# One bias for two heads: the row maxima of the latent softmax scaled and clamped in pairs

## The chip, the core and the metric

The kernel runs on one core of a Trainium2 chip. The metric is the device time of one execution in microseconds. Three runs of the kernel before gave 1462.78, 1457.17 and 1461.98 us: a median of 1461.98 us. One further execution was profiled; every duration below is from that one, which took 1457.81 us with a span of 1455.8 us.

## The reference, cut to what matters

One layer of a hybrid network works on 128 context tokens and 512 latent tokens, width 1024. One input projection feeds a two-way RWKV scan (branch A) and a windowed attention with 16 query heads in 4 groups, each group with its own keys and values (branch B); two output projections, sigmoid gates and a last projection merge them. The part in question is the attention of the latent queries, in blocks of 128 queries:

```python
def one(i):                                   # block i of 4
    s_loc = einsum('bhgqd,bhkd->bhgqk', qi, ki) * ATTN_SCALE      # window of up to 384 keys, masked
    s_ctx = einsum('bhgqd,bhkd->bhgqk', qi, k_ctx) * ATTN_SCALE   # 128 context keys
    pr = _sink_softmax(jnp.concatenate([s_loc, s_ctx], axis=-1), sink)
    return pr[..., :KSPAN] @ vi + pr[..., KSPAN:] @ v_ctx
```

The softmax has one extra column, the learned sink of the head, in its sum. The exponent is taken of the score less a maximum, so each row needs `-max(scale * row maximum, sink)` as its bias before the exponential can start.

## The kernel before, in words

All operations are recorded by one helper (line 138), so the trace shows one line for all and they are told apart by the names of their tiles. The scan and the input projections take the time to about 1106 us and are ordered by hand. What follows (from line 1603) is left to a list scheduler, which orders each engine's instructions by priority and by its own idea of their durations; the order is fixed when the program is built, and each engine then works strictly in that order.

From line 1623 a loop goes over the four head groups. For a group, `attend` (line 1293) makes the scores of its four heads against the context (one block, tile `Pc`), then four blocks of latent queries (tile `Pl`): blocks 0 and 3 have 384 keys, blocks 1 and 2 have 512. For each head of a block (line 1348): TensorE makes the scores in a PSUM tile `ur`, of which there are two (line 193), from the high and low parts of the keys (`KH`, `KL`) with queries `qt`, and adds the band mask with an identity product (`amask`, `identb`). VectorE takes the row maximum into one column of `nm` (line 1358), and scales and clamps it (line 1359); ScalarE reads `ur`, makes the exponential into `Pl` and its row sums in `ssum` (line 1364). Only then is that `ur` tile free for the head after next.

After four heads `softmax_tail` (line 1297) makes the reciprocals `den`, scales the four `Pl` on VectorE, and then for each 128 keys TensorE turns the four heads' pieces into one PSUM tile `sc` (a set of four transposes), ScalarE copies it out (`PT`), and TensorE multiplies it with the values (into `st` or `mi`). There is one `sc` tile, so a set waits for the copy of the set before. A group has 15 sets: one for the context block and 3, 4, 4 and 3 for the latent blocks; four groups have 60.

Two streams share the engines. Keys and queries of the next group are prepared in groups 0 to 2 (rotations `sh`, `R`, `us_q`, splits `qt`). And the projection of branch A (`branch_a`, 8 column blocks of 48 products, tiles `g` from `ah`, `al`, `wh`, `wl`) has the lowest priority: its products are the filler of TensorE. Two PSUM tiles `g` hold the two halves of a column block until VectorE has emptied them with `stg<-us_ma,g`; `us_ma` is loaded on SP's queue. After the attention, `branch_b` needs the gated outputs `bh`, `bl` of all groups (`yb` times `us_gb`, cast on ScalarE, low part on POOL), and `output` ends the kernel.

Of the kernel before, what the change touches and what calls it, by code (L numbers as in the profile page):

```python
# [15 lines left out]
AF = mybir.ActivationFunctionType  # L16
ALU = mybir.AluOpType
# [17 lines left out]
SCALE = 0.125  # L35
# [134 lines left out]
def hybrid_step(ctx, tc, a):  # L170
    nc = tc.nc
    clock = Clock()
    act, dve, pool_e, pe = (Timed(e, k, clock) for e, k in (
        (nc.scalar, "act"), (nc.vector, "dve"), (nc.gpsimd, "pool"), (nc.tensor, "pe")))
# [8 lines left out]
    def T(shape, tag, bufs, dt=F32, name=None):  # L183
        bufs = NB.get(tag, bufs)
        return sb.tile(shape, dt, tag=tag, name=name or tag, bufs=bufs)
# [6 lines left out]
    def PUR():  # L192
        return pools["ur"].tile([P, 512], F32, tag="ur", name="ur", bufs=2)
# [4 lines left out]
    def PSC():  # L198
        return psp.tile([P, 512], F32, tag="sc", name="sc", bufs=1)
# [15 lines left out]
    for tb in range(5):  # L215
# [13 lines left out]
                      in1=pv[:, :16].rearrange("p (c k) -> p c k", c=2), op=ALU.mult)  # L229
# [101 lines left out]
    for c in range(2):  # L331
        dve.tensor_tensor(out=mTf[:, c, :], in0=mTf[:, c, :], in1=vec("b_ada", 0, 16), op=ALU.add)
        dve.scalar_tensor_tensor(out=mTf[:, c, 8:16], in0=mTf[:, c, 8:16], scalar=1.0, in1=vec("norm_w", 0, 8),
                                 op0=ALU.add, op1=ALU.mult)
# [3 lines left out]
    for k in range(KB):  # L338
        hi = T([P, TOK], "h", 16, F32R, name="hh")
        for c, (t0, t1) in enumerate(((0, CTX), (CTX, TOK))):  # L340
            dve.tensor_scalar(out=xT[k][:, t0:t1], in0=xT[k][:, t0:t1], scalar1=mTf[:, c, 8 + k:9 + k],
                              scalar2=mTf[:, c, k:k + 1], op0=ALU.mult, op1=ALU.add)
# [203 lines left out]
    def unspill(nm, b, tag, bufs):  # L546
        t = T([P, TOK], tag, bufs, name="us_" + nm)
        nc.sync.dma_start(out=t, in_=spills[nm, b])
        return t
# [743 lines left out]
    def attend(g, Q, KH, KL, vt_, cv):  # L1293
        yb = [T([P, TOK], t, 1, name="yb") for t in ("bv", "DG")]
        hs = slice(4 * g, 4 * g + 4)

        def softmax_tail(Ps, nm, ssum, nk, vals, col0):
            den = T([P, 4], "den", 2, name="den")
            dve.tensor_tensor(out=den, in0=nm, in1=sink[:, hs], op=ALU.add)
            act.activation(out=den, in_=den, func=AF.Exp)  # L1300
            dve.tensor_tensor(out=den, in0=den, in1=ssum, op=ALU.add)
            dve.reciprocal(out=den, in_=den)
            for j in range(4):
                dve.tensor_scalar(out=Ps[j], in0=Ps[j], scalar1=den[:, j:j + 1], scalar2=None, op0=ALU.mult)
            po = (PST, PMI)[alt[0] % 2]()
            alt[0] += 1
            for kb in range(nk):
                pt = PSC()
                for j in range(4):
                    pe.transpose(out=pt[:, j * P:(j + 1) * P], in_=Ps[j][:, kb * P:(kb + 1) * P], identity=ident)  # L1310
                PT = T([P, 4, P], "SB", 10, name="PT")
                act.copy(out=PT.rearrange("p j x -> p (j x)"), in_=pt)
                for half in range(2):
                    pe.matmul(out=po[64 * half:64 * half + 64, 0:256], lhsT=vals[kb], rhs=PT[:, half::2, :],
                              start=(kb == 0), stop=(kb == nk - 1))
            for b in range(2):
                dve.tensor_copy(out=yb[b][:, col0:col0 + P], in_=po[:, b * P:(b + 1) * P])


        nm = T([P, 4], "nm", 2, name="nm")  # L1320
        ssum = T([P, 4], "ssum", 2, name="ssum")
        Ps = [None] * 4
        ps = PUR()
        for j in range(4):
            o = ps[:, j * P:(j + 1) * P]
            pe.matmul(out=o, lhsT=Q[j][:, 0:CTX], rhs=KH[:, 6 * P:], start=True, stop=False)
            pe.matmul(out=o, lhsT=Q[j][:, 0:CTX], rhs=KL[:, 6 * P:], start=False, stop=True)
        dve.tensor_reduce(out=nm, in_=ps.rearrange("p (j x) -> p j x", j=4), axis=AX.X, op=ALU.max)
        dve.scalar_tensor_tensor(out=nm, in0=nm, scalar=-SCALE, in1=nsink[:, hs], op0=ALU.mult, op1=ALU.min)
        Pt = T([P, 4, P], "S", 5, name="Pc")  # L1330
        for j in range(4):
            Pj = Pt[:, j]
            act.activation(out=Pj, in_=ps[:, j * P:(j + 1) * P], func=AF.Exp, scale=SCALE,
                           bias=nm[:, j:j + 1], accum_out=ssum[:, j:j + 1])
            Ps[j] = Pj
        softmax_tail(Ps, nm, ssum, 1, [vt_[0][:, CH * g:CH * g + CH]], 0)


        for i in range(4):
            b0, b1 = max(0, i - 1), min(3, i + 1)  # L1340
            nl = b1 - b0 + 1
            W = (nl + 1) * P
            c0 = 0 if i < 2 else P + P * b0
            f0 = P if i < 2 else 0
            nm = T([P, 4], "nm", 2, name="nm")
            ssum = T([P, 4], "ssum", 2, name="ssum")
            Ps = []
            for j in range(4):
                qs = Q[j][:, CTX + P * i:CTX + P * i + P]
                ps = PUR()  # L1350
                pe.matmul(out=ps[:, 0:W], lhsT=qs, rhs=KH[:, c0:c0 + W], start=True, stop=False)
                pe.matmul(out=ps[:, 0:W], lhsT=qs, rhs=KL[:, c0:c0 + W], start=False, stop=False)
                if i > 0:
                    pe.matmul(out=ps[:, f0:f0 + P], lhsT=identb, rhs=amask[:, 0, :], start=False, stop=(i == 3))
                if i < 3:
                    f1 = f0 + (nl - 1) * P
                    pe.matmul(out=ps[:, f1:f1 + P], lhsT=identb, rhs=amask[:, 1, :], start=False, stop=True)
                dve.tensor_reduce(out=nm[:, j:j + 1], in_=ps[:, 0:W], axis=AX.X, op=ALU.max)
                dve.tensor_scalar(out=nm[:, j:j + 1], in0=nm[:, j:j + 1], scalar1=-SCALE,
                                  scalar2=nsink[:, 4 * g + j:4 * g + j + 1], op0=ALU.mult, op1=ALU.min)  # L1360
                if j % 2 == 0:
                    Pt = T([P, 2, W], "S", 5, name="Pl")
                Pj = Pt[:, j % 2]
                act.activation(out=Pj, in_=ps[:, 0:W], func=AF.Exp, scale=SCALE, bias=nm[:, j:j + 1],
                               accum_out=ssum[:, j:j + 1])
                Ps.append(Pj)
            vals = [vt_[1 + b][:, CH * g:CH * g + CH] for b in range(b0, b1 + 1)]
            vals.insert(0 if i < 2 else nl, cv[:, g, :])
            softmax_tail(Ps, nm, ssum, nl + 1, vals, CTX + P * i)

        for b in range(2):
            sg = unspill("gb", 2 * g + b, "E", 1)
            if g < 3:
                bt = T([P, 2, TOK], ("bk", "ar", "ar")[g], 2, F32R, name="bt")
                bh, bl = bt[:, 0, :], bt[:, 1, :]
            else:
                bh = T([P, TOK], ("kk", "cs")[b], 1, F32R, name="bh")
                bl = T([P, TOK], ("rkv", "tmp")[b], 1, F32R, name="bl")
            dve.scalar_tensor_tensor(out=yb[b], in0=yb[b], scalar=0.5, in1=sg, op0=ALU.mult, op1=ALU.mult)
            act.copy(out=bh, in_=yb[b])  # L1380
            pool_e.tensor_tensor(out=bl, in0=yb[b], in1=bh.bitcast(F32), op=ALU.subtract)
            bhl.append((bh, bl))
# [230 lines left out]
    nsink = T([P, 16], "var", 1, name="nsink")  # L1613
# [9 lines left out]
    for g in range(4):  # L1623
        (KH, KL), Q = nxt
        if g < 3:
            nxt = whole(k_side(g + 1, kp)), whole(q_side(g + 1))
        attend(g, Q, KH, KL, vt_, cv)
        base = tc.cur_priority
        tc.cur_priority = 2000000 + base
        for _ in range(NBA[g]):  # L1630
            next(ba, None)
        tc.cur_priority = base + 2000
# [56 lines left out]
```

## Time and profile before

| what | value |
| --- | --- |
| runs, median (lowest to highest) | 1461.98 us (1457.17 to 1462.78) |
| profiled execution, its span | 1457.81 us, 1455.8 us |
| busy in the span: PE / DVE / ACT / POOL | 89% / 55% / 47% / 31% |
| attention, from its first score product to its last value product | 1106.7 to 1319.2 us |
| granted clock of the span | 0.952 of full speed |

PE is TensorE, PEld its weight loads, DVE VectorE, ACT ScalarE, POOL GpSimd, SP the queue that issues most transfers. A busy TensorE here means that a product was in the pipeline, not that the array was full. A waiting time in square brackets in a timeline is the idle time of the engine before the instruction and what ended it.

### The profile page before, as it was taken

The numbers are of one execution on the slowest core, as the hardware profiler recorded it, in microseconds if no ns is written. First come the engines' busy times: TensorE is split into PE (matmuls) and PEld (weight loads), VectorE is DVE, ScalarE is ACT, GpSimd is POOL, SyncE is SP. The second block draws the span as 40 slices with busy tenths as digits, with TensorE's granted clock in tenths as the row PEclk, the third lists the DMA queues.
The fourth block names the chain that finished last, engine by engine and source line by source line (L and its number), as shares of the span: only waits on it lengthen the run. The fifth ranks groups of instructions, "written<-read, shape, count | busy, mean of one in ns | idle before, by whom it ended". The sixth has DMA issues, their size and how long they took to land.

```text
span 1455.8 us, 40281 instructions
## 1 busy us (share of the span) xinstructions
PE 1301.2 (89%) x16959; PEld 1075.5 (74%) x16959; DVE 799.1 (55%) x1818; ACT 677.0 (47%) x1655; POOL 456.3 (31%) x476
## 2 busy tenths in 40 slices
PE   5699999989998999999998999999874789998996
PEld 0499888878887888887887887888553466777985
DVE  2436743665574475575465455437237787653447
ACT  2335364356356437436545645643433456553222
POOL 0333343224233233433332333332232122226330
PEclk9699999999999999999999999999885799999999
DMA  9133312223321321322231241233453222225532
GB/s 327 40 122 119 123 55 71 88 60 93 116 69 58 107 86 59 123 83 63 76 118 55 67 134 52 68 128 115 161 160 88 78 65 60 78 62 183 150 109 94
DMA packets 156722, 144.29 MB, mean 99 GB/s; under 512 B 16691, under 2 KB 130550, under 8 KB 156542
## 3 DMA queue, kind: packets, MB, share of 16 engines
q1 hardware_dynamic: 146632, 131.51, 28.9%
q10 hardware_dynamic: 9910, 10.21, 2.2%
q8 instruction: 133, 2.18, 0.6%
q14 instruction: 47, 0.39, 0.1%
HBM read 105.50 MB, written 36.18 MB: 97 GB/s over the span
## 4 chain that ended last, share of the span: by engine, by line
PE 69%; DVE 11%; issue 7%; ACT 5%; POOL 2%; DMA 1%; SPq 0%; DVEq 0%; ACTq 0%; POOLq 0%
PE g L138 39%; PE mi L138 11%; PE sc L138 7%; PE st L138 7%; PE ur L138 5%; DVE X L138 2%; DVE M L138 2%; ACT SB L138 1%; DVE Pl L138 1%; DVE St L138 1%; DVE o L138 1%; ACT L138 1%; DMA sp_rkv<-stg 1%; DVE stg L138 0%; DVE nm L138 0%
## 5 line engine op out<-in xcount | busy, mean ns | idle before, releaser
L138 POOL TENSOR_TENSOR wl<-wr,wh 128x512 fp32r<-128x512 f32 x170 | 229.2, 1352 | 637.7 <-ACT wh L138 599.2
L138 PE MATMUL g<-hh,wh 128*128 128x320 f32 (+1 forms) x1104 | 375.8, 340 | 9.9 <-DVE stg L138 4.9
L138 PE MATMUL g<-hl,wh 128*128 128x320 f32 (+1 forms) x1104 | 346.2, 314 | 5.1 <-issue 3.6
L138 PE MATMUL g<-hh,wl 128*128 128x320 f32 (+1 forms) x1104 | 345.7, 313 | 0.0
L138 PEld LDWEIGHTS g<-hh,wh 128*128 128x128 f32 x1104 | 210.8, 191 | 32.0 <-issue 7.8
L138 PEld LDWEIGHTS g<-hl,wh 128*128 128x128 f32 x1104 | 211.0, 191 | 5.7 <-issue 2.7
L138 PEld LDWEIGHTS g<-hh,wl 128*128 128x128 f32 x1104 | 211.8, 192 | 0.6
L138 ACT CAST wh<-wr 128x512 fp32r<-128x512 f32 x170 | 104.1, 618 | 17.3 <-PE g L138 11.3
L138 ACT COPY SB<-st 64x128 f32<-64x128 f32 x160 | 41.5, 260 | 144.0 <-PE st L138 142.8
L138 DVE SCALAR_TENSOR_TENSOR St<-St,pc,st 128x64 f32<-128x64 f32 x128 | 30.2, 277 | 124.1 <-PE st L138 100.3
L138 DVE SCALAR_TENSOR_TENSOR stg<-g,vt,stg 128x127 f32<-128x127 f32 (+1 forms) x144 | 60.8, 436 | 63.7 <-ACT stg L138 61.2
L138 ACT COPY U<-st 128x128 f32<-128x128 f32 x80 | 21.3, 266 | 136.4 <-DVE St L138 116.8
L138 POOL TENSOR_TENSOR S<-S,smask 128x512 f32<-128x512 f32 x40 | 50.8, 1271 | 98.9 <-ACT S L138 94.7
L138 PE MATMUL mi<-ar,bk 64*64 64x64 f32 (+1 forms) x960 | 71.9, 248 | 5.0 <-DVE XT L138 2.7
L138 ACT COPY SB<-sc 64x256 f32<-64x256 f32 (+1 forms) x160 | 55.2, 372 | 37.6 <-PE sc L138 36.4
L138 PEld LDWEIGHTS mi<-ar,bk 64*64 64x64 f32 (+1 forms) x960 | 61.9, 157 | 6.9 <-issue 2.9
L138 DVE TENSOR_TENSOR U<-ur,U 128x128 f32<-128x128 f32 x72 | 20.8, 289 | 77.3 <-PE ur L138 69.5
L138 ACT COPY PT<-sc 128x512 f32<-128x512 f32 x60 | 35.1, 584 | 47.9 <-PE sc L138 47.7
L138 DVE TENSOR_REDUCE nm<-ur 128x1 f32<-128x384 f32 (+2 forms) x68 | 41.4, 622 | 28.3 <-PE ur L138 28.0
L138 ACT ACTIVATE Pl<-ur,nm 128x384 f32<-128x384 f32 (+1 forms) x64 | 40.6, 635 | 28.1 <-DVE nm L138 25.5
L138 DVE TENSOR_TENSOR S<-sc,smask 128x512 f32<-128x512 f32 x40 | 27.3, 683 | 45.8 <-PE mi L138 24.9
L138 PE MATMUL g<-bt,wh 128*128 128x320 f32 x192 | 46.7, 320 | 5.3 <-DVE stg L138 5.3
(284 smaller groups left out, 2920.1 us busy)
## 6 DMA issues: line engine op xcount, KB each, us to landing
wr<-in_w_in SPq DMA_DIRECT2D x138, 256.0 KB
sp_rkv<-stg SPq DMA_DIRECT2D x48, 160.0 KB
rkv<-sp_rkv SPq DMA_DIRECT2D x24, 320.0 KB
wa_t<-in_w_ada SPq DMA_DIRECT2D x11, 512.0 KB
wg<-in_w_ada SPq DMA_DIRECT2D x16, 256.0 KB
wr<-in_w_oA SPq DMA_DIRECT2D x16, 256.0 KB
wr<-in_w_oB SPq DMA_DIRECT2D x16, 256.0 KB
wo<-in_w_out SPq DMA_DIRECT2D x16, 256.0 KB
```

The source lines that it names most:

```text
L138: return f(**kw)
```

## The change

The bias of two heads is made by one instruction. The maxima of heads 0 and 1 are taken first, then one `scalar_tensor_tensor` scales and clamps both columns of `nm`, then both exponentials follow; heads 2 and 3 likewise. The context block is as before (there all four columns were one instruction already), and so is everything else that the program asks for.

```diff
                 dve.tensor_reduce(out=nm[:, j:j + 1], in_=ps[:, 0:W], axis=AX.X, op=ALU.max)
-                dve.tensor_scalar(out=nm[:, j:j + 1], in0=nm[:, j:j + 1], scalar1=-SCALE,
-                                  scalar2=nsink[:, 4 * g + j:4 * g + j + 1], op0=ALU.mult, op1=ALU.min)
+                two.append(ps)
                 if j % 2 == 0:
                     Pt = T([P, 2, W], "S", 5, name="Pl")
-                Pj = Pt[:, j % 2]
-                act.activation(out=Pj, in_=ps[:, 0:W], func=AF.Exp, scale=SCALE, bias=nm[:, j:j + 1],
-                               accum_out=ssum[:, j:j + 1])
-                Ps.append(Pj)
+                    continue
+                dve.scalar_tensor_tensor(out=nm[:, j - 1:j + 1], in0=nm[:, j - 1:j + 1], scalar=-SCALE,
+                                         in1=nsink[:, 4 * g + j - 1:4 * g + j + 1], op0=ALU.mult, op1=ALU.min)
+                for b in range(2):
+                    act.activation(out=Pt[:, b], in_=two.pop(0)[:, 0:W], func=AF.Exp, scale=SCALE,
+                                   bias=nm[:, j - 1 + b:j + b], accum_out=ssum[:, j - 1 + b:j + b])
+                    Ps.append(Pt[:, b])
```

The scheduler answers with another order on every engine from the first group on. Three places of it matter below.

VectorE, in group 0, behind the rotation of the queries for group 1 (the piece begins with it); `nm` holds the maxima of latent block 0, `Pc` is the context block's softmax, `R` the keys of group 1:

```order
 L138 TENSOR_TENSOR us_q<-t_14965,sh 128x512
 L138 RECIPROCAL den<-den 128x4
-L138 TENSOR_SCALAR nm<-nm,nsink 128x1
-L138 TENSOR_SCALAR Pc<-Pc,den 128x128 x4
+L138 SCALAR_TENSOR_TENSOR nm<-nm,nsink 128x2
+L138 STREAM_SHUFFLE sh<-R 128x512
+L138 TENSOR_SCALAR Pc<-Pc,den 128x128
 L138 TENSOR_TENSOR qt<-us_q,qt 64x640 x2
```

The single bias becomes the pair's, and one rotation and the two query splits now stand ahead of three of the four scalings of the context block.

TensorE, in group 1, ahead of the four transposes of latent block 0 (`sc<-ident,Pl`); `g<-ah` and `g<-al` are products of branch A:

```order
 L138 MATMUL g<-al,wh 128x320
+L138 MATMUL g<-ah,wh 128x320
+L138 MATMUL g<-ah,wl 128x320
+L138 MATMUL g<-al,wh 128x320
+L138 MATMUL g<-ah,wh 128x320
+L138 MATMUL g<-ah,wl 128x320
+L138 MATMUL g<-al,wh 128x320
+L138 MATMUL g<-ah,wh 128x320
```

This piece is the head of a run: fifteen products of branch A stand now where one stood, between the scores of the next block's first two heads and the first transpose.

TensorE, at the end of group 3, the sets of its last blocks:

```order
 L138 MATMUL sc<-ident,Pl 128x128 x4
-L138 MATMUL g<-al,wh 128x320
-L138 MATMUL g<-ah,wh 128x320
-L138 MATMUL g<-ah,wl 128x320
-L138 MATMUL g<-al,wh 128x320
-L138 MATMUL g<-ah,wh 128x320
 L138 MATMUL mi<-PT,vtok 64x256 x2
 L138 MATMUL sc<-ident,Pl 128x128 x4
```

Here five products of branch A stood between a set of transposes and the values of the set before; now none does, at this place and in all the sets behind it.

## Rows read from the trace of the kernel before

**Rows 1.** Stretches, one per head group: length; busy PE, PEld, DVE, ACT, POOL; clock; DMA.

```profile
1106.70:1183.20 76.50, 50.62 (x258) 31.89 (x259) 63.25 (x155) 36.67 (x94) 16.98 (x11) 0.74 0.22 66
1183.20:1229.70 46.50, 41.66 (x248) 27.26 (x247) 36.47 (x95) 26.58 (x70) 14.16 (x10) 0.93 0.17 51
1229.70:1276.70 47.00, 45.99 (x302) 32.98 (x301) 31.17 (x92) 27.91 (x76) 12.14 (x9) 1.00 0.30 89
1276.70:1319.20 42.50, 41.99 (x280) 30.36 (x280) 21.86 (x67) 20.62 (x50) 8.30 (x6) 1.00 0.30 94
```

**Rows 2.** Groups by shape, 1106 to 1310 us, VectorE: busy us, mean ns | idle before.

```profile
L138 DVE TENSOR_REDUCE nm<-ur 128x1 f32<-128x512 f32 x32 | 21.6, 684 | 17.8 <-PE ur L138 17.8
...
L138 DVE TENSOR_SCALAR nm<-nm,nsink 128x1 f32<-128x1 f32 x64 | 11.9, 206 | 0.3
```

**Rows 3.** The same view for ScalarE.

```profile
L138 ACT ACTIVATE Pl<-ur,nm 128x512 f32<-128x512 f32 x32 | 22.0, 688 | 18.8 <-DVE nm L138 16.9 <-DVE den L138 1.8
...
L138 ACT ACTIVATION_READ_ACCUMULATOR Pl<-ur,nm 128x1 f32 x64 | 12.7, 198 | 0.0
```

**Rows 4.** Instructions on the tile nm: ns min/median/max of one.

```profile
L138 DVE SCALAR_TENSOR_TENSOR nm<-nm,nsink x4: 152/162/165, 1112.6 to 1267.2; 128x4 f32<-128x4 f32 x4
```

**Rows 5.** Waits of TensorE, 1106 to 1325 us: total, times, longest.

```profile
PE ur L138 <- ACT Pl L138: 10.9, 8, 5.5
```

**Rows 6.** Timeline of TensorE, full clock: values and transposes, without filler, then with.

```profile
1173.30 0.65 PE L138 MATMUL mi<-PT,vtok 128*64 128x256 f32 x4 [0.64 <-ACT PT L138]
1173.88 0.66 PE L138 MATMUL sc<-ident,Pl 128*128 128x128 f32 x4
1174.29 0.31 PE L138 MATMUL ur<-KH,qt 128*128 128x128 f32 x1
...
1175.21 0.65 PE L138 MATMUL mi<-PT,cv 128*64 128x256 f32 x4
...
1314.39 0.65 PE L138 MATMUL mi<-PT,vtok 128*64 128x256 f32 x4
...
1316.31 0.65 PE L138 MATMUL mi<-PT,vtok 128*64 128x256 f32 x4
```

**Rows 7.** Timeline of TensorE: values and transposes at half clock, two branch A products.

```profile
1145.49 1.12 PE L138 MATMUL mi<-PT,cv 128*64 128x256 f32 x4
1146.55 1.12 PE L138 MATMUL sc<-ident,Pl 128*128 128x128 f32 x4
...
1288.09 0.31 PE L138 MATMUL g<-al,wh 128*128 128x320 f32 x1
1288.23 0.31 PE L138 MATMUL g<-ah,wh 128*128 128x320 f32 x1
```

**Rows 8.** Timeline of VectorE, scaling of block 0 in group 1.

```profile
1187.46 4.54 DVE L138 TENSOR_SCALAR Pl<-Pl,den 128x384 f32<-128x384 f32 x4
```

**Rows 9.** Stretches around three thin places; columns as in rows 1.

```profile
1134.00:1144.00 10.00, 6.35 (x27) 3.86 (x25) 9.38 (x24) 3.98 (x11) 4.09 (x3) 0.84 0.29 85
1144.00:1151.00 7.00, 6.43 (x24) 3.27 (x24) 4.59 (x12) 2.32 (x7) 0.30 (x1) 0.57 0.00 0
1186.00:1192.00 6.00, 3.02 (x17) 1.64 (x15) 5.08 (x8) 2.05 (x5) 4.79 (x4) 0.92 0.35 107
1192.00:1198.20 6.20, 6.14 (x24) 4.33 (x24) 5.72 (x13) 3.24 (x7) 2.60 (x2) 0.53 0.30 86
1202.00:1208.00 6.00, 4.75 (x25) 2.44 (x25) 5.40 (x17) 2.81 (x7) 1.14 (x1) 1.00 0.01 3
```

**Rows 10.** Timeline of TensorE: first late set of group 3, then the end.

```profile
1294.28 0.28 PE L138 MATMUL sc<-ident,Pl 128*128 128x128 f32 x1
...
1318.50 0.65 PE L138 MATMUL mi<-PT,cv 128*64 128x256 f32 x4
...
1325.37 0.64 PE L138 MATMUL g<-bt,wh 128*128 128x320 f32 x1 [5.29 <-DVE stg L138]
...
1332.83 0.41 PE L138 MATMUL g<-bl,wh 128*128 128x320 f32 x1 [1.32 <-POOL bl L138]
```

More of the change, by code (lines that the diff above doesn't have):

```diff
@@ L1347, in attend @@
             Ps = []
+            two = []
             for j in range(4):
```

## The prediction

> **What bounds the kernel now.** I read the stretches first, one for each head group [rows 1]. TensorE is busy 50.62 of 76.5 us in group 0, 41.66 of 46.5 in group 1, 45.99 of 47.0 and 41.99 of 42.5 in groups 2 and 3; VectorE is busy 63.25, 36.47, 31.17 and 21.86 us there. So group 0 is held by VectorE and by latencies, at a mean granted clock of 0.74; groups 2 and 3 are held by TensorE; group 1 lies between. Then the waits of TensorE [rows 5]: 10.9 us in 8 places for an exponential that frees a score tile, the longest 5.5 us. Each instruction on the edited path stands in the groups by shape [rows 2 to 4]: a maximum over 512 keys takes 684 ns, a single bias 206 ns, a bias of four columns 162 ns, an exponential over 512 keys 688 ns and the read of its sum 198 ns. Last, the timeline of the sets [rows 6]: from one value product to the next it is 1.91 us with only small score products between (1173.30 to 1175.21) and 1.92 us with five products of branch A between (1314.39 to 1316.31). A set is therefore set by the single `sc` tile and its copy, and about five filler products hide in each set at no cost. This is what decides what the moved filler is worth.
>
> **The change part by part.** The sum starts from the profiled execution, 1457.8 us; the median of the runs is 4.2 us above it, and the forecast adds these 4.2 us again.
>
> Removed and added on VectorE. 64 biases of 206 ns go (13.2 us busy), 32 pair biases come. None with two columns stands in the trace; between a single one and one of four columns I take the nearer kind, the same instruction with four columns, 162 ns: 5.2 us. VectorE is relieved of 8.0 us, 2.0 us in each group. In groups 2 and 3 TensorE is the bound and this is worth nothing. In group 0 VectorE is full for most of the time and 2.0 us could come off, in group 1 as much again: bounds 0 and -4.0. I take -1.0, because the new order of group 0 puts a rotation and two splits ahead of three scalings, so what is saved is not on the chain there.
>
> The added wait. Head 0's exponential now waits for head 1's maximum, and its `ur` tile is held as long. With two such tiles no score of heads 2 and 3 can start before that. From the end of head 1's scores to the start of head 2's it is one maximum, the pair's bias and one exponential, 0.684 + 0.162 + 0.688 us, and hand-overs that I estimate at 0.1 us each from the starts in the timelines: 1.8 us (some 0.3 us less for 384 keys). It costs nothing where TensorE has that much other work standing between. I went through the new order and added up, at full clock, what stands there: about 0.145 us for a product of branch A (1288.09 to 1288.23 [rows 7]), 0.58 us for the values of a set (1173.30 to 1173.88) and 0.41 us for its transposes (1173.88 to 1174.29) [rows 6]. In 24 of the 28 places (7 in a group) it covers the need; in four it falls short, by 4.7 us in all: in blocks 0 and 1 of group 0, in block 2 of group 1 and in block 3 of group 3. The old order, counted in the same way with a single bias, falls short by 2.9 us. So this part costs +1.8 us. Queued behind the pair bias on VectorE are the scalings and rotations of the list; who waits for them is the next set of transposes. The bound on the bad side: in all 16 latent blocks the fourth head's sum comes one exponential and one sum read later (0.688 + 0.198 us), which nothing hides: 14.2 us. On the good side 0.
>
> The moved filler. Counted in the old order from the first score product, 46, 109 and 220 products of branch A have been issued by the first set of groups 1, 2 and 3, and 330 by the last set of all; in the new order 82, 168, 279 and 342. So 36 more go to group 0 and 23 more to group 1, and the filler is used up before the last ten sets of group 3. At 0.145 us the 59 products are 8.6 us. Where they land, TensorE is idle for 25.9 and 4.8 us [rows 1], and in group 1 fifteen stand in front of exactly the set whose scalings are slow, 4.54 us for four [rows 8]. I cost their new place at 0, with 8.6 us as the bound if the idle time there is not where they stand. What they leave: from the late set's last transpose (1294.28 + 0.28) to the end of the last value product (1318.50 + 0.65) are 24.6 us [rows 10]. Without filler they hold 0.67 us to the first value product (1173.88 + 0.66 to 1175.21 [rows 6]), ten sets of 1.92 us and 0.65 us for the last values, 20.5 us, and the score products of blocks 2 and 3 in between, whose pair must wait as above once inside a set (1.8 us) and once at its edge (I take 1.1 us): 23.4 us, thus -1.2 us, with bounds -4.1 and 0 at full clock.
>
> Behind the attention. TensorE waits 5.29 us for `stg`, and later 1.32 us for the last `bl` [rows 10]. The first stays: the old and the new order both load the last `us_ma` behind the second `us_gb`, which waits for `yb`. The second should go, since the casts and low parts of branch B's first weights no longer wait for the last filler: -1.3 us, bounds -1.3 and 0.
>
> Sum: -1.0 + 1.8 + 0 - 1.2 - 1.3 = -1.7 us, so 1456.1 us against 1457.8 us in a profiled execution, and 1460.3 us as a median.
>
> **The rivals.** First, the end at half clock. The last ten sets have gaps of 0.64 us and more [rows 6]. A thin stretch can be followed by half speed: 6.35 us busy of 10 us, then a clock of 0.57 (the two stretches from 1134 us [rows 9]); or not: 4.75 us of 6 us at 1.00 (from 1202 us [rows 9]). At half clock the values of a set take 1.06 us (1145.49 to 1146.55) instead of 0.58 us [rows 6, 7], the transposes likewise, about 1.0 us for a set. With eight sets hit it is +8.0 us, 1468.3 us. [...]
>
> Second, slower: latency. If VectorE is late at the pairs (its list has rotations between), the work that stands between does not line up with the wait, and the pair's extra exponential is exposed in all 16 blocks: 14.2 us instead of 1.8 us, thus 1472.7 us. It decides the sign from 10.8 us on, that is where 12 of the 16 blocks expose it (1460.3 - 1.8 + 10.8 = 1469.3 us, 0.5% above the median). For it speaks that ScalarE already waits 16.9 us for `nm` [rows 3]; against it the long filler runs of the new order. [...]
>
> Third, clearly faster: the slow place of group 1 goes. From 1186 to 1192 us TensorE is busy 3.02 of 6.0 us, and then runs 6.2 us at a clock of 0.53 [rows 9]. If the fifteen products fill the hole, 3.0 us of idle time go, and half of the next 6.14 busy us, 3.1 us: -6.1 us, 1454.2 us. Against it: VectorE's scalings are no faster for it, and the products may only come earlier.
>
> **How the numbers follow.** A difference below 0.5% (7.3 us) can't be told from none here. Forecast 0.41 (1460.3 us, no difference), end at half clock 0.14 (1468.3 us, still none), exposed latency 0.20 (slower), slow place gone 0.25 (faster). So faster 0.25, none 0.55, slower 0.20. The range for 8 in 10 reaches nearly to the exposed latency, 1472 us, and, below the third rival by the rest of VectorE's bound (3.0 us) and a little of the late sets', to 1450 us; the forecast's own is 1454 to 1467 us.
>
> **What would show it.** The pair bias at 150 to 200 ns, 32 times. TensorE's waits for `Pl` on `ur` at 10 to 15 us. In group 1, no scaling wait above 0.5 us ahead of the first latent block, if the third rival is right. In the last ten sets, value products 1.9 us apart at a clock of 1.00; 2.9 us apart means the half clock. About 23 us from the late set to the end. The wait for `bl` gone, the one for `stg` still there. I am wrong if groups 0 to 2 together differ by more than 5 us from 170.0 us, or if the end takes longer than 26 us.

## The result and the profile after

The changed kernel is slower: 1470.82 us in the median of six runs (1468.17 to 1475.61) against 1462.17 us of the kernel before beside it (1456.43 to 1462.78), a ratio of 1.0073, with a 95% interval from 1.0049 to 1.0096. The forecast was 1460.3 us and no difference. The profiled execution took 1470.82 us with a span of 1469.0 us, 13.2 us more than the span before; the medians differ by 8.7 us and the means by 10.6, so some 2 to 5 us of what follows belong to the single executions.

The stretches first, one per head group, from the first score product to the end of the last value product, cut as in [rows 1] at the transposes of the next group's context block (so the scores of a group's block 0 mostly stand in the stretch before), columns as there:

```profile
1105.10:1185.60 80.50, 53.03 (x294) 35.61 (x295) 63.00 (x146) 37.09 (x96) 20.02 (x13) 0.75 0.25 74
1185.60:1240.10 54.50, 48.30 (x273) 31.91 (x273) 38.83 (x91) 27.81 (x73) 14.89 (x10) 0.87 0.19 59
1240.10:1289.50 49.40, 45.64 (x294) 32.97 (x294) 32.03 (x78) 25.54 (x68) 11.74 (x8) 0.97 0.24 71
1289.50:1334.70 45.20, 36.05 (x230) 23.28 (x230) 24.48 (x62) 21.63 (x53) 8.62 (x6) 1.00 0.25 77
```

Every group is longer than in [rows 1]: by 4.0, 8.0, 2.4 and 2.7 us, 17.1 us in all. The part ahead of the attention is 1.6 us shorter, the part behind it 2.3 us. TensorE's busy time over the four groups is 183.0 us against 180.3 for about as many products (1091 in the trace against 1088), at a lower granted clock in groups 1 and 2 (0.87 against 0.93, 0.97 against 1.00), so the attention did not get more work: of the 17.1 us, 14.3 us are new idle time. The idle time does not stand where the length does, since the filler moved forward: group 1 is 8.0 us longer with 1.4 us more idle time and 25 more products in the trace, group 3 only 2.7 us longer with 8.6 us more idle time and 50 fewer products.

The waits of TensorE from 1106 to 1340 us (total, times, longest), which answer to [rows 5]; first one more row of the kernel before, then the changed kernel:

```profile
PE sc L138 <- DVE Pl L138: 5.7, 8, 1.2
```

```profile
PE sc L138 <- DVE Pl L138: 14.5, 13, 3.2
PE sc L138 <- DVE Pc L138: 10.1, 2, 9.9
...
PE ur L138 <- ACT Pl L138: 3.9, 6, 1.8
```

The wait that the change was to lengthen, a score tile `ur` held by its exponential, fell from 10.9 to 3.9 us. What grew is the wait of the transposes for the scaled `Pl`, 14.5 us against 5.7 us before. (The 9.9 us for `Pc` stand at the start of group 0 and cost nothing: the first copy of `sc` starts at 1132.5 us before and 1132.6 us after.) The engines ahead of TensorE show where that lateness comes from. The groups by shape on VectorE and ScalarE (busy us, mean ns | idle time before, and what ended it), as in [rows 2, 3], with the instructions on `nm` as in [rows 4]:

```profile
L138 DVE TENSOR_REDUCE nm<-ur 128x1 f32<-128x512 f32 x32 | 21.7, 683 | 25.9 <-PE ur L138 25.8
L138 DVE TENSOR_REDUCE nm<-ur 128x1 f32<-128x384 f32 x32 | 17.5, 551 | 14.8 <-PE ur L138 14.7
L138 DVE SCALAR_TENSOR_TENSOR nm<-nm,nsink 128x2 f32<-128x2 f32 x32 | 7.5, 233 | 0.5
...
L138 ACT ACTIVATE Pl<-ur,nm 128x512 f32<-128x512 f32 x32 | 22.0, 691 | 28.0 <-DVE nm L138 24.1 <-PE g L138 3.9
```

```profile
L138 DVE SCALAR_TENSOR_TENSOR nm<-nm,nsink x36: 127/160/1240, 1111.0 to 1322.4; 128x2 f32<-128x2 f32 x32, 128x4 f32<-128x4 f32 x4
```

The maxima over 512 keys now wait 25.8 us for scores (17.8 before), the exponentials 24.1 us for their bias (16.9 before). So the scores themselves come later, although TensorE is hardly seen waiting for a score tile. As I read it, the scheduler knew of the wait when it fixed the order, and put the scores behind other work; that would be why the row of the wait is small.

One block shows it, the first latent block of group 3, at a clock of 1.00 in both. Before, from the timelines of TensorE, VectorE and ScalarE (start, us, operation, idle time before it and its releaser):

```profile
1266.29 0.39 PE L138 MATMUL ur<-KH,qt 128*128 128x384 f32 x1
1268.29 0.56 DVE L138 TENSOR_REDUCE nm<-ur 128x1 f32<-128x384 f32 x1 [0.71 <-PE ur L138]
1270.01 0.60 ACT L138 ACTIVATE Pl<-ur,nm 128x384 f32<-128x384 f32 x1
1270.27 0.34 PE L138 MATMUL ur<-KH,qt 128*128 128x384 f32 x1
1271.05 0.34 PE L138 MATMUL ur<-KH,qt 128*128 128x384 f32 x1
```

And after:

```profile
1281.74 0.39 PE L138 MATMUL ur<-KH,qt 128*128 128x384 f32 x1
1285.95 0.34 PE L138 MATMUL ur<-KH,qt 128*128 128x384 f32 x1
1286.57 0.56 DVE L138 TENSOR_REDUCE nm<-ur 128x1 f32<-128x384 f32 x1 [1.71 <-PE ur L138]
1287.17 0.16 DVE L138 SCALAR_TENSOR_TENSOR nm<-nm,nsink 128x2 f32<-128x2 f32 x1
1287.42 0.58 ACT L138 ACTIVATE Pl<-ur,nm 128x384 f32<-128x384 f32 x1 [1.02 <-DVE den L138]
1288.32 0.34 PE L138 MATMUL ur<-KH,qt 128*128 128x384 f32 x1
```

The score products shown are those of heads 0, 1 and 2. Before, head 0 had its exponential at 1270.01, so head 2's scores could follow head 1's by 0.78 us. After, head 0 has its maximum by 1283.1, in VectorE's timeline, but its exponential only when head 1's scores, 4.2 us later, have passed the maximum and the pair's bias; head 2 then starts 2.37 us behind head 1. Head 1 is as late in both (4.0 us behind head 0 before), because its tile still held the context block's scores; what the pair adds is that head 0's tile stays held until then, from 1281.74 to 1288.00, 6.3 us against 4.3 us before. Over the 16 latent blocks, head 0's tile is held for 5.50 us before and 6.85 us after, from its first score product to the end of its exponential, and head 2's scores start 0.4 us behind that end in the mean of both: it is the tile that they wait for, seen or unseen.

The interval from one head's scores to the next head's was read in the timelines of the runs, as the mean over the 16 latent blocks; this table was worked out from the starts of the score products (means in us; "next" is the first head of the next block).

| kernel | head 0 to 1 | 1 to 2 | 2 to 3 | 3 to next |
| --- | --- | --- | --- | --- |
| before | 3.39 | 2.50 | 3.74 | 2.91 |
| after | 2.04 | 5.16 | 1.56 | 4.93 |

The scores come in bursts of two. From the first head of the first latent block to the first head of the sixteenth it is 210.3 us, against 192.3 us before: 14.0 us for a block against 12.8, and 18.0 us in all, about the 17.1 us by which the attention grew.

### The profile page after: what moved, and what is told of

The parts are those of the page before. It is cut to its first block, busy times and chain, and to the rows that moved or that the text cites. A ratio compares the mean times of both kernels' runs of the same rounds, so it can differ in the third digit from the quotient of the medians.

```text
span 1469.0 us, 40251 instructions
## 1 busy us (share of the span) xinstructions
PE 1307.0 (89%) x16959; PEld 1076.7 (73%) x16959; DVE 804.7 (55%) x1786; ACT 676.7 (46%) x1655; POOL 456.7 (31%) x476
## 4 chain that ended last, share of the span: by engine, by line
PE 68%; DVE 13%; issue 8%; ACT 5%; POOL 1%; DMA 0%; DVEq 0%; ACTq 0%; POOLq 0%
PE g L138 39%; PE mi L138 11%; PE sc L138 7%; PE st L138 7%; PE ur L138 5%; DVE X L138 2%; DVE M L138 2%; DVE Pl L138 1%; DVE nm L138 1%; ACT SB L138 1%; DVE St L138 1%; DVE o L138 1%; DVE stg L138 1%; DVE qt L138 1%; ACT L138 0%
## 5 line engine op out<-in xcount | busy, mean ns | idle before, releaser
L138 PE MATMUL sc<-ident,Pl 128*128 128x128 f32 x224 | 45.3, 302 | 14.7 <-DVE Pl L138 14.5
L138 PEld LDWEIGHTS sc<-ident,Pl 128*128 128x128 f32 x224 | 26.4, 146 | 37.6 <-issue 24.0
```

The costliest lines, as they stand in the source:

```text
L138: return f(**kw)
```

## The experiments

Each run is given as a ratio to the kernel before on the same chip, with its 95% interval; before was 1454.7 to 1457.1 us in these rounds. The times in the first expectations start from 1462.2 us, so compare ratios. The theories stand in the expectations; A comes from the late transposes of the changed kernel's trace, which pointed to the fourth head's sum.

**Which part of the change costs.** e1 keeps the writing in pairs but makes two single biases; e2 keeps single heads but takes the new kind of instruction; e3 and e4 pair only the first or the last two heads.

```diff
e1 (in the change)
-                dve.scalar_tensor_tensor(out=nm[:, j - 1:j + 1], in0=nm[:, j - 1:j + 1], scalar=-SCALE, ...)
+                for b in range(2):
+                    c = j - 1 + b
+                    dve.tensor_scalar(out=nm[:, c:c + 1], in0=nm[:, c:c + 1], scalar1=-SCALE, ...)
e2 (in before)
-                dve.tensor_scalar(out=nm[:, j:j + 1], in0=nm[:, j:j + 1], scalar1=-SCALE, ...)
+                dve.scalar_tensor_tensor(out=nm[:, j:j + 1], in0=nm[:, j:j + 1], scalar=-SCALE, ...)
e3, e4 (the change under a condition, the old lines else)
+                if j < 2:        # e4: if j >= 2:
```

> Written in pairs as the change is (both maxima, then both biases, then both exponentials), but the two biases are made by two single instructions, so no exponential depends on the other head's maximum. Before is 1462.2 us and the change 1470.8 us. Theory A (the dependence: the fourth head's exponential and row sum come later, and the four scalings and the first transposes of a block with them): no dependence is left, 1460 to 1465 us, waits of TensorE for the scalings of Pl near the 15 us of before (14.9) rather than the 24.6 of the change for Pl and Pc. Theory C (no dependence, but the other order: every rewriting moves the filler of branch A forward, here 103 products by the seventeenth set where before had 56 and the change 113): 1468 to 1473 us. Theory D (the kind of the instruction, 233 ns for a pair): 1462 us, as before.

> As before, head by head, but each single bias is made by the kind of instruction that the change uses (scalar_tensor_tensor on one column). Theory A: nothing waits for a second head, so 1460 to 1465 us, whatever the order. Theory C: the filler stands forward here too (97 products by the seventeenth set, 120 by the twentieth, where before had 56 and 78), so 1468 to 1473 us. Theory D: the kind costs about 64 times the difference to 206 ns; at 150 to 230 ns that is -3.6 to +1.5 us busy and under 1.5 us of time.

> Only heads 0 and 1 of a block share a bias; heads 2 and 3 have single ones. Theory A: the fourth head's sum waits for no other head, so most of the loss is gone: 1460 to 1465 us. Theory B (the two score tiles are held longer, so that the scores of heads 2 and 3 start late): the loss is all here, 1468 to 1472 us, since only the first pair's tiles are waited for by scores of the same block. Theory C: the filler is as far forward as in the change (103 by the seventeenth set, used up by the fiftieth), so 1468 to 1473 us.

> Only heads 2 and 3 share a bias; heads 0 and 1 have single ones. Theory A: the fourth head's sum comes as late as in the change: 1468 to 1473 us. Theory B: 1462 to 1465 us. Theory C: the filler stands further forward than in any other (141 products by the twentieth set, where before had 78), so 1468 to 1475 us.

Measured: e1 0.9995 (0.9977 to 1.0013), e2 0.9962 (0.9940 to 0.9984), e3 1.0061 (1.0037 to 1.0084), e4 1.0009 (0.9988 to 1.0031). Theory A falls by e3 and e4, which came out the wrong way round for it; theory C by e1 and e2, where the filler stands as far forward and nothing is lost; theory D by e2. What is left is B: the first pair carries the loss. From head 1's scores to head 2's it is 3.27 us in e1, 3.71 in e2, 3.64 in e4, but 5.26 us in e3. The last pair holds its tiles too: in e4 the next block's first head comes 4.81 us behind head 3, against 2.91 us before. But the block as a whole takes 13.1 us there and 13.4 us in e3, against 12.8 us before, 12.9 in e1 and 12.3 in e2; the time per block goes with the cost better than any one interval.

**A third tile, and no filler.** The third tile takes the place of `st`; the filler is taken away by tying its first input to the last gated output.

```diff
e5, e6
-        return pools["ur"].tile([P, 512], F32, tag="ur", name="ur", bufs=2)
+        return pools["ur"].tile([P, 512], F32, tag="ur", name="ur", bufs=3)
-            po = (PST, PMI)[alt[0] % 2]()
-            alt[0] += 1
+            po = PMI()
e7, e8 (in part; branch_a runs behind the four groups)
+            if k == 0:
+                dve.tensor_copy(out=hi[:, 0:1], in_=hold[-1][:, 0:1])
+                dve.tensor_copy(out=lo[:, 0:1], in_=hold[-1][:, 0:1])
```

> The change with three score tiles instead of two; the bank is taken from the tile st, so that the values of every set go to mi. To be read against the next run, the same without the pairs. After the first four runs theory A (late sum of the fourth head) is down, since pairing the last two heads cost nothing and pairing the first two cost 0.6%. Theory B (a pair holds both score tiles until its bias and first exponential are done, so that the scores of heads 2 and 3 start late): with a third tile head 2 waits for nothing of the pair, so this kernel is within 4 us of the next one. Theory C2 (which order the scheduler happens to find decides, plus or minus 0.5% whatever the pairs): the difference is anything up to 7 us of either sign.

> The control: the kernel before with three score tiles and without st. In its order only 78 products of branch A stand ahead of group 2, and 121 are left for after the attention, so the attention is shorter by up to 121 x 0.145 = 17.5 us and the work behind it longer by as much; in all 1450 to 1462 us.

> The change, with the whole projection of branch A moved behind the attention (its first tile waits for the last gated output), so that no filler covers a wait in the attention. To be read against the next run, the same without the pairs. Theory B: nothing but sets stands in the wait between the scores of heads 1 and 2, so the difference to the next run is larger than the 10.7 us that the change shows with filler: 12 to 25 us, all of it in the attention. Theory C (the filler that the change moves forward is the cost): no filler is there to move, so 0 to 3 us. The time itself is some 342 x 0.145 = 50 us longer than with filler, less what the attention becomes shorter: 1480 to 1510 us.

> The control: the kernel before with the projection of branch A behind the attention: 1475 to 1500 us.

Measured: e5 0.9998 (0.9978 to 1.0018), e6 0.9852 (0.9825 to 0.9878); e7 1.0425 (1.0394 to 1.0455), e8 1.0421 (1.0393 to 1.0449). e6 is 16 us faster than the fastest that I expected, e7 and e8 are 8 and 16 us slower than the slowest. Both comparisons went against theory B as it then stood. With three tiles the pairs cost more, not less, and without filler nothing that can be measured, though head 2 comes 4.48 us behind head 1 in e7 and 3.21 us in e8; a block takes 13.1 and 12.9 us there. Without filler TensorE's granted clock is lower too (the second, third and fourth group of e8, from one context block's first copy to the next):

```profile
1176.74:1224.58 47.84, 35.97 (x185) 19.49 (x185) 34.37 (x96) 26.03 (x68) 9.54 (x6) 0.86 0.08 22
1224.58:1271.58 47.00, 37.62 (x184) 19.98 (x184) 27.36 (x83) 22.45 (x62) 6.26 (x4) 0.78 0.10 26
1271.58:1314.48 42.90, 30.93 (x156) 15.88 (x156) 21.21 (x64) 19.04 (x49) 3.09 (x2) 0.88 0.13 40
```

The mean granted clock of these groups was 0.86, 0.78 and 0.88; before, they had 0.93, 1.00 and 1.00 [rows 1]. The values of a set took 1.12 us at one place of e8's third group (1250.80) and 0.65 us at another (1253.27). The same two times stand in the kernel before, 1.12 us at a granted clock of 0.50 (1145.45 to 1147.60 us, around the first line of [rows 7]) and 0.65 us at 1.00 (1173.30 to 1176.00 us, the first part of [rows 6]). That this gives the softmax the time that it lacks otherwise is a guess; no run shows it by itself, and why the pairs cost nothing without filler stays open.

**The filler metered, and another order.** In e9 and e10 the third and sixth column block of branch A may start only behind groups 1 and 2, in both kernels alike. e11 is the change with the two score products of a head swapped, e12 is e6 with the instruction of e2.

```diff
e9, e10
                 t[3] = T([P, KB, P], "wl", 2, F32R, name="wl")
+                if held:
+                    act.copy(out=t[2][:, 0, 0:1], in_=held.pop()[:, 0:1])
...
+            if j in (2, 5):
+                held.append(bhl[-1][0].bitcast(F32))
             gemm(a["w_oA"][0], P * j, xh, xl, ev)
e11
-                pe.matmul(out=ps[:, 0:W], lhsT=qs, rhs=KH[:, c0:c0 + W], start=True, stop=False)
-                pe.matmul(out=ps[:, 0:W], lhsT=qs, rhs=KL[:, c0:c0 + W], start=False, stop=False)
+                pe.matmul(out=ps[:, 0:W], lhsT=qs, rhs=KL[:, c0:c0 + W], start=True, stop=False)
+                pe.matmul(out=ps[:, 0:W], lhsT=qs, rhs=KH[:, c0:c0 + W], start=False, stop=False)
```

> The change with the filler metered: the weights of branch A's third and sixth column block wait for the last gated output of groups 1 and 2 (a copy of one column ties them). Its products stand then at 54, 54, 125 and 243 by the last set of groups 0 to 3 (the change: 80, 166, 275 and 342), and the next run, the same without pairs, has 40, 54, 126 and 224. Theory B (the pair's hold of the score tiles lengthens the chain of the softmax itself): the difference between the two stays as large as between the change and before, 7 to 12 us. Theory C3 (the hold is harmless; the loss is that the filler, called in early to cover it, stands ahead of the chain in groups 0 to 2 and is used up in group 3, where TensorE is then idle 8.4 us): with equal filler the difference is under 3 us.

> The control: the kernel before with the same metering. Theory B for the attention as a whole (its length is set by the softmax chain, and filler is carried along for nothing): the attention ends where it did, or earlier, though 106 fewer products are done in it, and those cost 106 x 0.145 = 15.4 us behind it, less the 5 us in which TensorE waits for stg there: about 1465 us. If TensorE sets the length, the time stays at 1457 us.

> The change, with each score's product of the low key part issued ahead of the one of the high part: the same work and the same number of products, another order from the scheduler in many places. Theory C2 (which order the scheduler finds decides, by 0.5% either way): anything from 1450 to 1475 us. Theories B and C3: the loss stays, 0.4 to 1.0% over before.

> The kernel before with three score tiles, and each head's own bias made by scalar_tensor_tensor on one column, which took 176 ns against 206 ns of tensor_scalar. Both edits had shown less time by themselves (1.5% and 0.4%); if they add, 1428 to 1430 us against 1457 us; if the second was the luck of an order, 1432 to 1440 us.

Measured: e9 1.0147 (1.0119 to 1.0175), e10 1.0005 (0.9983 to 1.0027), e11 1.0100 (1.0066 to 1.0134), e12 0.9881 (0.9851 to 0.9911). With nearly equal filler (243 products by the last set in e9, 224 in e10) the pairs cost 1.4%, so the filler that moved forward is not the cost; it may have paid for a part. The loss stays in another order (e11, where head 2 comes 5.07 us behind head 1). e10 came out 8 us better than I expected: with 106 products less in it the attention itself became shorter (205.2 us against 212.5), so there the filler was not all free. The pair's mark is there again: 5.00 us from head 1 to head 2 in e9, 2.35 us in e10. e12 is no faster than e6, so a part of what e2 gained was its order and not the 30 ns by which its bias is shorter (176 against 206 ns); orders alone seem to be worth about 0.4%.

**The hold by itself.** e13 holds the first tile of two heads until the second bias is there, and delays no exponential; e14 has the same operations without the hold; e15 takes one tile away.

```diff
e13 (in before, behind the bias of head j; e14 reads ps in the place of last)
+                if j % 2:
+                    act.activation(out=ssum[:, j:j + 1], in_=last[:, 0:1], func=AF.Copy, scale=nm[:, j:j + 1])
+                last = ps
e15
-        return pools["ur"].tile([P, 512], F32, tag="ur", name="ur", bufs=2)
+        return pools["ur"].tile([P, 512], F32, tag="ur", name="ur", bufs=1)
```

> The kernel before (single biases, early exponentials), with one small ScalarE operation added for each two heads: it reads one element of the first head's score tile with the second head's bias as its factor (its result is overwritten), so that the first tile stays held until the second bias, as in the change, while its exponential is made early, as before. The next run has the same 32 operations without the hold. Theory B (the hold): 0.5 to 1.0% slower than the next run, TensorE idle 8 us or so in group 3. Theory E (not the hold, but that the exponentials and sums themselves come later): within 0.2% of the next run.

> The control: the same 32 small operations, each reading the second head's own tile, which its exponential holds anyway. 32 x 0.2 = 6.4 us more busy time of ScalarE, which is busy 47%: 1456 to 1464 us against 1456 us.

> The kernel before with one score tile instead of two (a bank is left unused). What a score tile is worth: three instead of two gave -1.5%. If a pair costs what one tile costs (three tiles with pairs ran like two without, 0.9998), two with pairs, 1.0073, should be about what one is without pairs: 1464 to 1475 us. If a tile is worth more the fewer there are, 1480 us and more.

Measured: e13 1.0081 (1.0056 to 1.0107), e14 1.0019 (1.0000 to 1.0038), e15 1.0647 (1.0616 to 1.0679). The hold alone makes 0.6%, nearly the whole of the change's 0.7%, with the exponentials as early as before: head 0's ends 5.15 us behind the start of its scores in e13, 5.50 us in the kernel before. But head 2's scores start 2.83 us behind that end in e13, and 0.63 us in e14; head 2 follows head 1 by 5.42 us in e13 and by 3.28 us in e14. The added operation takes 262 ns in the median in e13, where I had estimated 0.2 us. Over the whole span the mean granted clock is 0.946 in e13 and 0.947 in e14, but over the four groups it is 0.86, 0.94, 1.00 and 0.93 against 0.88, 1.00, 1.00 and 1.00; how much of the difference that makes is not shown. The last group, from its context block's first copy to its last copy, shows idle time of TensorE as in the change, in e13 and then in e14:

```profile
1286.57:1331.19 44.62, 35.98 (x205) 21.36 (x203) 25.55 (x66) 21.93 (x57) 7.01 (x5) 0.93 0.21 67
```

```profile
1283.15:1323.30 40.15, 35.73 (x235) 24.40 (x233) 23.09 (x63) 21.23 (x53) 8.27 (x6) 1.00 0.28 85
```

With fewer products (205 against 235) e13 takes 44.62 us for it where e14 takes 40.15, and TensorE is idle for 8.64 us of these against 4.42. Theory E falls. The difference of 0.6% is not far above the 0.4% by which orders alone seem to differ, so it does not stand alone: all five kernels that hold the first pair's tile with two tiles and filler (the change, e3, e9, e11, e13) lose 0.6 to 1.5%, and none of the five with two tiles and filler that do not (e1, e2, e4, e10, e14) loses more than 0.2%. e15 shows that a pair does not cost what a tile does: the second tile is worth 6.5%.

**Three tiles once more.** e3 and e4 with the edit of e6.

> Three score tiles, and only heads 0 and 1 share a bias. By theory B a third tile moves the wait on by one head: with two tiles head 2's scores wait for the first pair, with three head 3's do (in e5 head 3's scores start 4.74 us after head 2's on average, without pairs, e6, 1.92 us). So the first pair should carry most of the 1.5% between e6 and e5: 1446 to 1456 us against 1434 us of e6, with 4 us or more from head 2's scores to head 3's. If the loss is not the wait for the first pair's tile, 1432 to 1440 us.

> Three score tiles, and only heads 2 and 3 share a bias. By theory B head 3's tile comes free with head 0's early exponential, so nothing of the block waits for a pair: 1432 to 1442 us, 2 to 2.5 us from head 2's scores to head 3's. If any pair costs with three tiles, 1446 us and more.

Measured: e16 0.9934 (0.9910 to 0.9958), e17 0.9948 (0.9930 to 0.9966), against 0.9852 of e6 and 0.9998 of e5. The wait did move on to the next head: from head 2's scores to head 3's it is 1.92 us in e6, 4.74 in e5, 3.89 in e16 and 2.30 in e17, and the first pair costs 0.8%. But the last pair costs 1.0% there, which I had expected to be near nothing. With three tiles either pair costs. The timelines offer a reason for the last one: with three tiles head 2's goes to head 1 of the next block, and from head 0's scores to head 1's it is 3.16 us in e17 against 1.92 us in e6. That this is the whole of it no run shows.

**The version that beats both** is e6: three tiles and single biases, 1434.10 us (1430.68 to 1437.60) against 1457.10 us. Its four groups, from one context block's first copy of `sc` to the next, and the part behind the last copy, in its profiled execution:

```profile
1126.93:1169.11 42.18, 37.66 (x215) 23.61 (x216) 36.49 (x101) 26.57 (x70) 8.53 (x6) 0.89 0.21 64
1169.11:1211.10 41.99, 40.06 (x265) 26.91 (x264) 36.34 (x106) 28.87 (x78) 11.80 (x8) 1.00 0.17 51
1211.10:1251.92 40.82, 37.05 (x244) 24.74 (x243) 32.47 (x85) 24.33 (x67) 12.16 (x8) 1.00 0.28 83
1251.92:1284.60 32.68, 32.24 (x213) 21.56 (x212) 20.52 (x60) 18.11 (x44) 5.65 (x4) 1.00 0.21 65
...
1284.60:1428.90 144.30, 130.62 (x773) 119.83 (x771) 70.46 (x181) 39.65 (x80) 52.76 (x38) 0.98 0.45 145
```

The same four groups take 185.2 us in the kernel before and 157.7 us here. Groups 2 and 3 of before, in which TensorE was busy for 98% and more of the time [rows 1], shrink too: what filled TensorE there was filler, and 121 of the 384 products of branch A are now left at the last set, against 12 in the kernel before. The part behind grows by only 6.2 us to the span's end, though 109 products more are some 15.8 us (an estimate at 0.145 us each): the waits for `stg` and `bl` of [rows 10], 6.6 us together, are gone. The part ahead of the first copy is 5.6 us shorter too.

## Why the prediction was wrong, point by point

**What bounds the kernel: wrong.** I read a busy TensorE in groups 2 and 3 as the bound. Its last few per cent of idle time were taken by work of the lowest priority, which can stand anywhere. The length of each group is set by the chain of scores, maximum, bias, exponential and the tile that it frees; e6 shortens all four groups although the work as a whole is the same, and e13 lengthens the attention against e14 (225.4 us against 214.3), which has the same operations. That the pairs cost nothing without filler (e7, e8) does not follow from this, and is open.

**The added wait: the step that failed.** "It costs nothing where TensorE has that much other work standing between" is the sentence. The count behind it may well have been right: TensorE did not stand still for the tile (3.9 us, where I had forecast 10 to 15). But work that covers a wait does not shorten it for those who come behind; the next scores, the maxima and the transposes were later all the same. Where the prediction had +1.8 us, the attention shows +17.1 us in the profiled execution, and the hold alone 8.6 us in the medians (e13 against e14). I had also priced the wait as 1.8 us of hand-overs behind head 1's scores, and left out that head 1's scores themselves come late (2.0 us behind head 0 in the mean, 4.2 us in the block above), so that head 0's tile is held for all of that.

**VectorE, -1.0 us: not seen.** The pair's bias has a median of 160 ns, as forecast (162), but three of the 32 last 780 to 1240 ns, and the mean is 233 ns; 4.4 us of busy time were saved (11.9 less 7.5), not 8.0. The forecast had also taken 64 means for the busy time, 13.2 us, where [rows 2] has 11.9. Nothing of it shows: group 0, where I had looked for it, has VectorE busy for 63.00 us as against 63.25.

**The moved filler, 0 us: right for another reason.** With nearly equal filler the change loses more (e9, e10), so that its new place may have been worth something. That it is used up early lets TensorE's idle time show in group 3; it is not what makes the kernel slower.

**The late sets, -1.2 us: right in size; the part behind, -1.3 us: right in sign.** From the first late set's last transpose (1310.79 + 0.27) to the end of the last value product are 23.6 us, where 23.4 had been forecast, at a clock of 1.00; the value products at the end are 1.91 to 1.97 us apart:

```profile
1310.79 0.27 PE L138 MATMUL sc<-ident,Pl 128*128 128x128 f32 x1
...
1326.27 0.65 PE L138 MATMUL st<-PT,vtok 128*64 128x256 f32 x4 [0.67 <-ACT PT L138]
1328.18 0.65 PE L138 MATMUL st<-PT,cv 128*64 128x256 f32 x4 [0.68 <-ACT PT L138]
...
1333.98 0.65 PE L138 MATMUL mi<-PT,cv 128*64 128x256 f32 x4 [0.73 <-ACT PT L138]
1341.17 0.64 PE L138 MATMUL g<-bt,wh 128*128 128x320 f32 x1 [6.54 <-DVE stg L138]
```

The wait for `stg` stayed and grew from 5.29 to 6.54 us, the one for `bl` [rows 10] is gone, and the part behind the attention is 2.3 us shorter, more than the bound of 1.3. The size of the late sets is in part luck: of the 2.9 us that I gave to two waits of a pair, nearly all (2.3 us) stands in one place, between the value products at 1318.17 and 1322.39, where the transposes wait for the scaled `Pl`.

**The rivals.** The end at half clock did not come: the granted clock was 1.00 from 1289.50 to 1334.70 us, though TensorE was busy for only 36.05 of 45.20 us there. The slow place of group 1 did not go; the group became 8.0 us longer. The exposed latency came, and close to its price (1472.7 us forecast, 1470.8 measured), but not at the place that I gave for it, so that the nearness is luck: I had put the price on the fourth head's sum, and the last pair is free with two tiles (e4), while the first one costs (e3). Grouping lost 0.7% here, with VectorE busy for 24.48 to 38.83 us of 45.2 to 54.5 in groups 1 to 3, and two single biases lost none (e1, 0.9995). But it is not the size of the operation that costs, since e13 loses as much with single biases (1.0081). My own criterion, over 5 us in groups 0 to 2 together, was met by 14.4 us (184.4 against 170.0).

## What to carry to other kernels

A busy engine is the bound only if what keeps it busy has to be done there; look at which instructions fill it, and treat the lowest priority's as idle time. When an edit lets one result wait for another, ask which buffer is held meanwhile and who writes it next, and price the time until the second operand is there, not only the operations between. And a scheduler that knows of a wait can hide the wait's row: compare when the chain's own instructions start, not how long anyone is seen waiting.

## What the runs showed of the hardware

VectorE's scaling of `Pl` by a column, four of 384 elements, took 1.40 us where POOL was idle, and about 1.1 us for each one where a product or difference of two tiles ran on POOL nearly all the time (4.54 us for four [rows 8], 3.38 us for three below). Of the 16 such groups of four in the two profiles, the eight without a POOL instruction beside them take about 0.35 us for each scaling, the other eight 0.44 to 1.23 us; why is not shown. First the kernel before, group 3; then the changed kernel at the same block, with POOL's instructions:

```profile
1280.50 1.40 DVE L138 TENSOR_SCALAR Pl<-Pl,den 128x384 f32<-128x384 f32 x4
```

```profile
1295.58 3.38 DVE L138 TENSOR_SCALAR Pl<-Pl,den 128x384 f32<-128x384 f32 x3
1299.08 1.23 DVE L138 TENSOR_SCALAR Pl<-Pl,den 128x384 f32<-128x384 f32 x1
...
1295.60 1.53 POOL L138 TENSOR_TENSOR wl<-wr,wh 128x512 fp32r<-128x512 f32 x1 [2.43 <-ACT wh L138]
1297.09 1.65 POOL L138 TENSOR_TENSOR bt<-yb,bt 128x640 fp32r<-128x640 f32 x1
1298.71 1.39 POOL L138 TENSOR_TENSOR wl<-wr,wh 128x512 fp32r<-128x512 f32 x1
```

This is 3.2 us on the chain in one block (4.61 us for the four against 1.40 us), and the 4.54 us of [rows 8] agree with it: POOL is busy for 4.79 us of the 6.0 us around them [rows 9]. Which blocks are hit is a matter of the order, and may be a part of the 0.4% by which orders differ. The second score tile was worth 6.5% (e15, 1.0647), the third 1.5% (e6, 0.9852), this one net of the value tile `st` that was given up for it.
